# SwiGLU's result: transposing it in 32x32 blocks on VectorE and GpSimd instead of on TensorE

## The chip, the cores and the metric
The kernel runs on one core of one Trainium2 chip. A core has five engines that work side by side: TensorE (matrix products; PE in the profile, with its weight loads as PEld), VectorE (DVE), ScalarE (ACT), GpSimd (POOL) and SyncE (SP, whose queue issues the loads here). The metric is the device time of one execution in microseconds (us), the median of several runs.

## The reference, cut to what matters
One decoder layer on 256 tokens with D = 2048: a SwiGLU FFN (half step), a token mixer, and a second SwiGLU FFN (half step). Each sub-layer has a norm before and behind it, modulated by vectors (adaLN) that come from a product of c with w_ada.

```python
def swiglu(h, w_gate, w_up, w_down):
    return (jax.nn.silu(h @ w_gate) * (h @ w_up)) @ w_down

x = sublayer(x, 0, ffn(0), 0.5)
x = sublayer(x, 1, mixer, 1.0)
x = sublayer(x, 2, ffn(1), 0.5)
```

D_FF is 5632, so each FFN has three weight matrices of 46 MB in float32. All inputs are float32.

## The kernel before, in words
**Three products for one.** A float32 matrix product is made of three products of fp32r operands: each operand is split into a high part (a cast) and a low part (the operand less the high part). `mm3` (L333) issues them on L334, L335 and L336. For a weight tile, `split_w` (L308) has ScalarE cast the raw tile to wh (L315) and VectorE subtract it to get wl (L316); for an activation, `split_act` does the same (L369, L370).

**Weights.** `load_w` (L302) loads a raw tile of 128 x 2 x 512 numbers (2 k-chunks of 128 rows, 512 columns; 512 KB) through SyncE's queue into the pool rawp, tag "raw", which has 8 buffers. wh and wl have 4 buffers each (pool wsp). `w_tiles` goes through a weight matrix in such tiles; I call the work on one raw tile a step. After each step it calls `pump()` (L285), which advances the first of the pending pieces of work by one `yield`, and `side[0].step()`, which advances the adaLN sums by a certain rate. `flush()` runs all that is pending to its end.

**The adaLN sums.** `ada_sums` loads tiles of w_ada into the same 8 raw buffers and VectorE adds them up, scaled by the activated c (L171). Most of them lie in the first FFN, where the rate is about 0.66 tiles for each step.

**An FFN.** D_FF is cut into 11 blocks of 512 columns, and these into three groups (`supers`): 4, 4 and 3 blocks. For a block, the gate and the up product are made token by token into two PSUM banks each (`proj_tok`: tokens on partitions, 128 x 512 for each of two token tiles t); that is 8 steps for each product, fewer in the first FFN, where part of the sums was made ahead. Then `swiglu_evac` or, with sums made ahead, `swiglu_sum` makes silu(gate) * up as two tiles gts[t] of 128 tokens x 512 columns. Those pieces are pending, and are pumped during the steps of the next block: the multiplications behind its first step, the transposition behind its third and fourth. The down product needs the result with columns on partitions, so `to_g` (L532) transposes it: for each half of the 512 columns four transposes of 128x128 on TensorE (L538) into a PSUM bank, and then `split_act` into g, high and low. When all blocks of a group have their g, the down product runs over them, four quarters of 512 output columns each.

**What sets the order.** The program is written in order, and a planner in the framework puts the instructions of each engine's queue in their order when the program is built, by its own reckoning of when each is ready; waits between engines are put in by it. Buffers belong to tags: raw (8), t2 (6, used for sg and gt of SwiGLU, for g_post, and other short-lived tiles), wh and wl (4).

Of the kernel before, what the change touches and what calls it, by code (L numbers as in the profile page):

```python
# [8 lines left out]
F32 = mybir.dt.float32  # L9
# [5 lines left out]
P = 128  # L15
D = 2048
S = 256
NT = S // P
# [14 lines left out]
def tile_layer(  # L33
# [6 lines left out]
    nc = tc.nc  # L40
# [14 lines left out]
    rawp = ctx.enter_context(tc.tile_pool(name="rawp", bufs=8))  # L55
# [9 lines left out]
    def nm(s):  # L65
        uid[0] += 1
        return f"{s}_{uid[0]}"

    def ps():
        return psp.tile([P, 512], F32, tag="ps", name=nm("ps"))  # L70

    def t2(shape=(P, 512), dtype=F32):
        return tp.tile(list(shape), dtype, tag="t2", name=nm("t2"))
# [203 lines left out]
    pending = []  # L277

    def later(fn, *args):
        def one():  # L280
            fn(*args)
            yield
        pending.append(one())
# [11 lines left out]
    def flush():  # L295
        while pending:
            pump()
# [35 lines left out]
    def mm3(o, lh, ll, rh, rl, start, stop):  # L333
        nc.tensor.matmul(o, lh, rh, start=start, stop=False, skip_group_check=True)  # L334
        nc.tensor.matmul(o, lh, rl, start=False, stop=False, skip_group_check=True)  # L335
        nc.tensor.matmul(o, ll, rh, start=False, stop=stop, skip_group_check=True)  # L336
# [20 lines left out]
    def proj_tok(src, c0, begun=None, w=512, segs=FULL, banks=None, first=0):  # L357

        if begun is not None:
            banks, segs = begun[0], FULL[begun[1]:]  # L360
        banks = banks or [ps(), ps()]
        last = segs[-1][0] + segs[-1][1] - 1
        for k, wh, wl in w_tiles(src, segs, c0, w=w):
            for t in range(NT):
                tok_mm(k, wh, wl, t, banks[t][:, 0:w], first, last)
        return banks

    def split_act(dh, dl, src):
        act = nc.scalar.copy(dh, src)  # L369
        return nc.vector.tensor_tensor(out=dl, in0=src, in1=dh.bitcast(F32), op=ALU.subtract), act  # L370


    def parts():

        p = small((P, 8), "parts")
        nc.gpsimd.memset(p[:, 3:4], EPS)
        return p

    def sumsq(p, q, src):
        junk = t2()  # L380
        nc.scalar.activation(junk, src, AF.Square, scale=float(D) ** -0.5, accum_out=p[:, q + q // 3:q + q // 3 + 1])  # L381
# [81 lines left out]
    def early_w(src, c0, w):  # L463


        if src is None:
            return None
        tiles = []
        for half, h in enumerate((hh, hl)):
            raw = load_w(src, 2 * half, c0, w)  # L470
            v = h[:, 8:16, :].rearrange("p (a j u) s -> p a j (u s)", a=2, j=2)
            wh, wl = split_w(raw[:, :, 0:w], v, w)
            tiles += [(2 * half + j, wh[:, j, :], wl[:, j, :]) for j in range(2)]
        return tiles
# [54 lines left out]
        return banks, 2  # L529


    def to_g(g, gts):  # L532
        for i in range(2):
            pg = ps()
            for j in range(2):
                for t in range(NT):
                    m = 2 * i + j
                    nc.tensor.transpose(pg[:, j * S + t * P:j * S + (t + 1) * P], gts[t][:, m * P:(m + 1) * P], ident)  # L538
            split_act(g.t[:, 0, 2 * i:2 * i + 2, :], g.t[:, 1, 2 * i:2 * i + 2, :],
                      pg.rearrange("p (k s) -> p k s", s=S))  # L540
            yield

    def swiglu_evac(g, gb, ub):
        gts = []
        for t in range(NT):
            sg, gt = t2(), t2()
            nc.scalar.activation(sg, gb[t], AF.Silu)
            nc.vector.tensor_tensor(out=gt, in0=sg, in1=ub[t], op=ALU.mult)
            gts.append(gt)
        yield  # L550
        yield
        yield from to_g(g, gts)

    def swiglu_sum(gb, ub, part):

        pv = part.t.rearrange("p k s -> p (k s)")
        gts = []
        for t in range(NT):
            sg, gt = t2(), t2()
            nc.vector.tensor_tensor(out=sg, in0=pv[:, t * 512:(t + 1) * 512], in1=gb[t], op=ALU.add)  # L560
            nc.scalar.activation(sg, sg, AF.Silu)
            nc.vector.tensor_tensor(out=gt, in0=pv[:, 1024 + t * 512:1024 + (t + 1) * 512], in1=ub[t], op=ALU.add)
            nc.vector.tensor_tensor(out=gt, in0=sg, in1=gt, op=ALU.mult)
            gts.append(gt)
        part.free()
        g = Slot((P, 2, 4, S), F32R)

        def rest():
            yield
            yield  # L570
            yield from to_g(g, gts)

        pending.append(rest())
        return g

    def ffn(idx, supers, begun, xin, nxt, nxt_src=None, nxt_c0=None, nxt_w=512):

        y = None
        yp = [parts() for _ in range(NT)]

        def evac_y(si, q, t, bank):
            ys = y[t].t[:, q * 512:(q + 1) * 512]
            if si == 0:
                nc.scalar.copy(ys, bank)
            else:
                nc.vector.tensor_tensor(out=ys, in0=ys, in1=bank, op=ALU.add)  # L586
            if si == len(supers) - 1:
                sumsq(yp[t], q, ys)

        for si, blocks in enumerate(supers):  # L590
            gs = []
            n = len(blocks)
            for b, segs, part, banks in blocks:
                if si == 0 and begun is not None and not gs:
                    gb = proj_tok(w_ff_gate[idx], b * FB, begun)
                    ub = proj_tok(w_ff_up[idx], b * FB)
                elif part is not None:
                    gb = proj_tok(w_ff_gate[idx], b * FB, segs=segs, first=segs[0][0])
                    ub = proj_tok(w_ff_up[idx], b * FB, segs=segs, first=segs[0][0])
                    flush()  # L600
                    gs.append(swiglu_sum(gb, ub, part))
                    continue
                else:
                    gb = proj_tok(w_ff_gate[idx], b * FB, segs=segs, banks=banks and banks[0])
                    ub = proj_tok(w_ff_up[idx], b * FB, segs=segs, banks=banks and banks[1])
                flush()
                gs.append(Slot((P, 2, 4, S), F32R))
                pending.append(swiglu_evac(gs[-1], gb, ub))
            if y is None:
                y = [Slot((P, D)) for _ in range(NT)] if xin[0].__class__ is Half else [Half(t) for t in range(NT)]  # L610
            rows = [(4 * i, 4, 4 * b[0]) for i, b in enumerate(blocks)]

            def mms(k, wh, wl, t):
                g = gs[k // 4].t
                mm3(banks[t], g[:, 0, k % 4, t * P:(t + 1) * P], g[:, 1, k % 4, t * P:(t + 1) * P],
                    wh, wl, k == 0, k == 4 * n - 1)

            for q in range(4):
                banks = [ps(), ps()]
                if si == len(supers) - 1 and q == 2:  # L620
                    for s_ in xin:
                        s_.t
                if si == len(supers) - 1 and q == 3:
                    flush()
                    if side[0] is not None:
                        side[0].drain()
                    early = early_w(nxt_src, nxt_c0, nxt_w)
                    kept, slots = hold(w_ff_down[idx], rows, q * 512, NW if nxt is None else 3)

                    def last_mm(t):  # L630
                        for k, wh, wl in kept:
                            mms(k, wh, wl, t)

                    return boundary(last_mm, lambda t: evac_y(si, q, t, banks[t]), lambda t: times_gg(y, t, q), xin, y, yp, slots + gs,
                                    early, 1, nxt, nxt_src, nxt_c0, nxt_w)
                else:
                    for k, wh, wl in w_tiles(w_ff_down[idx], rows, q * 512):
                        for t in range(NT):
                            mms(k, wh, wl, t)
                    for t in range(NT):  # L640
                        later(evac_y, si, q, t, banks[t])
                        if si == len(supers) - 1:
                            later(times_gg, y, t, q)
            if si < len(supers) - 1:
                for g in gs:
                    g.free()
# [72 lines left out]
    for bs, n in (((0, 1, 2, 3, 4), 1), ((5, 6), 2), ((7,), 3)):  # L719
        first.until(n - 1)  # L720
        for b in bs:
            part = Slot((P, 8, S))
# [32 lines left out]
    blocks = [(4718, 410), (4308, 410), (3896, 412), (3484, 412), (G0, 412)]  # L755
# [387 lines left out]
```

## Time and profile before

| | |
|---|---|
| median of 3 runs | 1872.65 us (1872.63 to 1873.1) |
| the profiled execution | 1873.27 us |
| its span, first to last instruction | 1871.5 us |
| granted TensorE clock, mean | 0.999 |
| TensorE busy | 1821.6 us (97%) |
| VectorE busy | 1366.2 us (73%) |
| ScalarE busy | 853.0 us (46%) |
| GpSimd busy | 17.8 us (1%) |
| DMA, mean over the span | 267 GB/s |

The first FFN lies between about 20 and 780 us, the mixer up to about 1140 us, the second FFN behind it. A row with x is a group of instructions with their count. Busy times of an engine are those of its instructions; matmuls are pipelined, so a matmul of 0.39 us starts 0.23 us behind the one before it. An engine executes its queue in order, and an instruction that waits keeps those behind it waiting.

### The profile page before, as it was taken

The numbers are of one execution on the slowest core, as the hardware profiler recorded it, in microseconds if no ns is written. First come the engines' busy times: TensorE is split into PE (matmuls) and PEld (weight loads), VectorE is DVE, ScalarE is ACT, GpSimd is POOL, SyncE is SP. The second block draws the span as 40 slices with busy tenths as digits, with TensorE's granted clock in tenths as the row PEclk, the third lists the DMA queues.
The fourth block names the chain that finished last, engine by engine and source line by source line (L and its number), as shares of the span: only waits on it lengthen the run. The fifth ranks groups of instructions, "written<-read, shape, count | busy, mean of one in ns | idle before, by whom it ended". The sixth has DMA issues, their size and how long they took to land.

```text
span 1871.5 us, 23045 instructions
## 1 busy us (share of the span) xinstructions
PE 1821.6 (97%) x8493; PEld 1522.8 (81%) x8493; DVE 1366.2 (73%) x1483; ACT 853.0 (46%) x1058; POOL 17.8 (1%) x40
## 2 busy tenths in 40 slices
PE   3999999999999999999999999999999999999998
PEld 2888888888888888799988887888888888888886
DVE  6788798788987888868898987555556555556455
ACT  3545444444443444655545446444444444334443
POOL 0000000000000000000000000000000000000000
PEclk9999999999999999999999999999999999999999
DMA  9999889989899999588689994776777776677652
GB/s 356 335 361 346 306 297 319 317 311 321 291 335 322 340 304 340 183 240 280 219 287 310 355 344 140 221 221 213 228 228 220 222 224 217 217 228 219 187 191 90
DMA packets 232617, 499.82 MB, mean 267 GB/s; under 512 B 16828, under 2 KB 28332, under 8 KB 231992
## 3 DMA queue, kind: packets, MB, share of 16 engines
q1 hardware_dynamic: 232504, 498.36, 80.0%
q8 instruction: 66, 1.08, 0.2%
q14 instruction: 47, 0.39, 0.1%
HBM read 496.19 MB, written 2.10 MB: 266 GB/s over the span
## 4 chain that ended last, share of the span: by engine, by line
PE 86%; issue 8%; DVE 3%; DMA 2%; POOL 1%; ACT 0%; DVEq 0%; POOLq 0%; ACTq 0%
PE ps L334 28%; PE ps L335 28%; PE ps L336 28%; DVE acc L171 1%; PE ps L538 1%; DMA raw<-in_w_ff_up_dram 1%; DVE wl L316 1%; DMA raw<-in_w_ada_dram 0%; POOL rstd L387 0%; DMA xt<-in_x_dram 0%; DMA raw<-in_w_ff_gate_dram 0%; PE ps L930 0%; POOL brs L808 0%; PE ps L436 0%; PE ps L230 0%
## 5 line engine op out<-in xcount | busy, mean ns | idle before, releaser
L316 DVE TENSOR_TENSOR wl<-raw,wh 128x1024 fp32r<-128x1024 f32 (+2 forms) x637 | 768.6, 1210 | 453.7 <-ACT wh L315 453.0
L315 ACT CAST wh<-raw 128x1024 fp32r<-128x1024 f32 (+2 forms) x637 | 662.7, 1043 | 865.3 <-PE ps L336 742.5
L334 PE MATMUL ps<-wh,hh 128*128 128x512 f32 (+2 forms) x1680 | 652.1, 390 | 3.0 <-ACT hh L369 2.4
L335 PE MATMUL ps<-wl,hh 128*128 128x512 f32 (+2 forms) x1680 | 649.4, 387 | 1.2 <-DVE wl L316 1.2
L336 PE MATMUL ps<-wh,hl 128*128 128x512 f32 (+2 forms) x1680 | 649.7, 387 | 0.0
L334 PEld LDWEIGHTS ps<-wh,hh 128*128 128x128 f32 x1680 | 316.2, 189 | 62.2 <-ACT hh L369 3.0
L335 PEld LDWEIGHTS ps<-wl,hh 128*128 128x128 f32 x1680 | 316.6, 188 | 61.2 <-DVE wl L316 2.6
L336 PEld LDWEIGHTS ps<-wh,hl 128*128 128x128 f32 x1680 | 316.1, 188 | 60.4
L171 DVE SCALAR_TENSOR_TENSOR acc<-raw,cs,acc 128x1024 f32<-128x1024 f32 x270 | 345.1, 1278 | 0.8 <-DVE parts L385 0.4
L334 PE MATMUL ps<-wh,big 128*128 128x512 f32 x804 | 314.8, 392 | 0.0
L335 PE MATMUL ps<-wl,big 128*128 128x512 f32 x804 | 313.3, 390 | 0.2 <-DVE wl L316 0.2
L336 PE MATMUL ps<-wh,big 128*128 128x512 f32 x804 | 313.3, 390 | 0.0
L335 PEld LDWEIGHTS ps<-wl,big 128*128 128x128 f32 x804 | 151.1, 188 | 31.6 <-DVE wl L316 1.1
L336 PEld LDWEIGHTS ps<-wh,big 128*128 128x128 f32 x804 | 151.0, 188 | 31.6
L334 PEld LDWEIGHTS ps<-wh,big 128*128 128x128 f32 x804 | 150.9, 188 | 30.7
L680 ACT COPY big<-ps 128x512 f32<-128x512 f32 x32 | 18.7, 589 | 45.4 <-PE ps L336 44.3
L334 PE MATMUL ps<-hh,wh 128*128 128x256 f32 x128 | 37.6, 294 | 0.0
L370 DVE TENSOR_TENSOR big<-ps,big 128x512 fp32r<-128x512 f32 x52 | 35.5, 683 | 1.3 <-ACT big L369 1.2
L336 PE MATMUL ps<-hh,wl 128*128 128x256 f32 x128 | 36.2, 283 | 0.0
L335 PE MATMUL ps<-hl,wh 128*128 128x256 f32 x128 | 36.2, 283 | 0.0
L369 ACT CAST big<-ps 128x512 fp32r<-128x512 f32 x52 | 30.1, 578 | 0.0
L381 ACT ACTIVATE t<-xt 128x512 f32<-128x512 f32 x32 | 20.0, 626 | 17.8 <-DVE xt L586 9.8
(196 smaller groups left out, 742.6 us busy)
## 6 DMA issues: line engine op xcount, KB each, us to landing
raw<-in_w_ada_dram SPq DMA_DIRECT2D x224, 512.0 KB, 5.4
raw<-in_w_ff_gate_dram SPq DMA_DIRECT2D x176, 512.0 KB, 4.6
raw<-in_w_ff_up_dram SPq DMA_DIRECT2D x176, 512.0 KB, 4.5
raw<-in_w_ff_down_dram SPq DMA_DIRECT2D x176, 512.0 KB, 5.2
raw<-in_w_ada_dram SPq DMA_DIRECT2D x128, 256.0 KB, 5.4
raw<-in_w_in_dram SPq DMA_DIRECT2D x48, 512.0 KB, 5.0
raw<-in_w_out_dram SPq DMA_DIRECT2D x32, 512.0 KB
raw<-in_w_in_dram SPq DMA_DIRECT2D x24, 412.0 KB, 5.1
```

The lines of the kernel that those rows point to most:

```text
L171: ins = nc.vector.scalar_tensor_tensor(a, raw[:, j, :, :], cs[:, k:k + 1], a, op0=ALU.mult, op1=ALU.add)
L315: behind(nc.scalar.copy(wh, rawv), floor[1])
L316: last_split[0] = nc.vector.tensor_tensor(out=wl, in0=rawv, in1=wh.bitcast(F32), op=ALU.subtract)
L334: nc.tensor.matmul(o, lh, rh, start=start, stop=False, skip_group_check=True)
L335: nc.tensor.matmul(o, lh, rl, start=False, stop=False, skip_group_check=True)
L336: nc.tensor.matmul(o, ll, rh, start=False, stop=stop, skip_group_check=True)
L369: act = nc.scalar.copy(dh, src)
L370: return nc.vector.tensor_tensor(out=dl, in0=src, in1=dh.bitcast(F32), op=ALU.subtract), act
L381: nc.scalar.activation(junk, src, AF.Square, scale=float(D) ** -0.5, accum_out=p[:, q + q // 3:q + q // 3 + 1])
L538: nc.tensor.transpose(pg[:, j * S + t * P:j * S + (t + 1) * P], gts[t][:, m * P:(m + 1) * P], ident)
L680: nc.scalar.copy(part.t.rearrange("p k s -> p (k s)")[:, u * 1024 + i * 512:u * 1024 + (i + 1) * 512], banks[i])
```

## The change
For all blocks of a group but the last, `to_g_blocks` takes the place of `to_g`. VectorE transposes each 128x512 tile gts[t] in one instruction, in blocks of 32x32, which leaves each block on the partitions that it came from. GpSimd then copies the blocks to the partitions where they belong: for each of 4 x 4 pairs of source and target partition groups one copy of 32 partitions x 256 numbers, 16 in all. Then come four yields, and the two splits, which read the SBUF tile gf instead of a PSUM bank. tr and gf are tiles of the tag "raw", of the size of a raw tile. The transposes and the copies stand one pump behind the multiplications, the splits at the fifth and sixth pump behind that. The last block of each group goes through `to_g` as before.

```diff
+    def to_g_blocks(g, gts):
+        tr = rawp.tile([P, NT, 4, 4, 32], F32, tag="raw", name=nm("tr"))
+        gf = rawp.tile([P, 4, NT, 4, 32], F32, tag="raw", name=nm("gf"))
+        for t in range(NT):
+            nc.vector.transpose(tr[:, t].rearrange("p m q r -> p (m q r)"), gts[t])
+        for b in range(4):
+            for q in range(4):
+                nc.gpsimd.tensor_copy(gf[q * 32:(q + 1) * 32, :, :, b, :].rearrange("p m t r -> p t m r"),
+                                      tr[b * 32:(b + 1) * 32, :, :, q, :])
+        for _ in range(4):
+            yield
+        for i in range(2):
+            split_act(g.t[:, 0, 2 * i:2 * i + 2, :], g.t[:, 1, 2 * i:2 * i + 2, :],
+                      gf[:, 2 * i:2 * i + 2].rearrange("p m t b r -> p m (t b r)"))
+            yield
...
-    def swiglu_evac(g, gb, ub):
+    def swiglu_evac(g, gb, ub, blocks):
...
         yield
-        yield
-        yield from to_g(g, gts)
...
+        if blocks:
+            yield from to_g_blocks(g, gts)
+        else:
+            yield
+            yield from to_g(g, gts)
...
-                    gs.append(swiglu_sum(gb, ub, part))
+                    gs.append(swiglu_sum(gb, ub, part, len(gs) + 1 < n))
...
-                pending.append(swiglu_evac(gs[-1], gb, ub))
+                pending.append(swiglu_evac(gs[-1], gb, ub, len(gs) < n))
```

`swiglu_sum` takes the same flag and branches in the same way.

## Rows read from the trace of the kernel before

**Rows 1.** The page: busy time, share of the span, instructions of each engine.
```profile
PE 1821.6 (97%) x8493; PEld 1522.8 (81%) x8493; DVE 1366.2 (73%) x1483; ACT 853.0 (46%) x1058; POOL 17.8 (1%) x40
```
**Rows 2.** Busy time by stretch (us), granted clock, DMA share, GB/s.
```profile
200.00:300.00 100.00, 100.00 (x475) 82.42 (x474) 89.95 (x101) 47.84 (x57) 0.00 (x0) 1.00 0.86 290
...
400.00:500.00 100.00, 100.00 (x466) 82.30 (x465) 88.06 (x96) 44.11 (x48) 0.00 (x0) 1.00 0.90 305
...
1300.00:1500.00 200.00, 200.00 (x895) 165.64 (x894) 111.67 (x103) 86.80 (x93) 0.00 (x0) 1.00 0.72 222
```
**Rows 3.** Waits of the engines and of SyncE's queue: us, times, longest.
```profile
ACT wh L315 <- PE ps L336: 742.5, 465, 2.4
...
SPq L304 <- DVE wl L316: 895.7, 463, 20.6
```
**Rows 4.** Timeline, TensorE around four transposes: start, us, engine, line, operation.
```profile
228.78 0.39 PE L335 MATMUL ps<-wl,hh 128*128 128x512 f32 x1
...
229.00 0.39 PE L336 MATMUL ps<-wh,hl 128*128 128x512 f32 x1
...
229.24 0.60 PE L538 MATMUL ps<-ident,t 128*128 128x128 f32 x4
...
229.91 0.40 PE L335 MATMUL ps<-wl,hh 128*128 128x512 f32 x1
```
**Rows 5.** Groups by line and shape: count | busy us, mean ns of one.
```profile
L316 DVE TENSOR_TENSOR wl<-raw,wh 128x1024 fp32r<-128x1024 f32 x599 | 730.5, 1222 | 435.3 <-ACT wh L315 434.7
...
L171 DVE SCALAR_TENSOR_TENSOR acc<-raw,cs,acc 128x1024 f32<-128x1024 f32 x270 | 345.1, 1278 | 0.8 <-DVE parts L385 0.4
...
L369 ACT CAST big<-ps 128x512 fp32r<-128x512 f32 x52 | 30.1, 578 | 0.0
L538 PE MATMUL ps<-ident,t 128*128 128x128 f32 x176 | 26.3, 272 | 0.0
...
L182 DVE STREAM_TRANSPOSE t<-acc 128x512 f32<-128x512 f32 x22 | 14.6, 691 | 0.1
...
L369 ACT CAST hh<-t 128x512 fp32r<-128x512 f32 x14 | 8.3, 621 | 0.1
```
**Rows 6.** Timeline, second FFN: a block's two SiLUs and its multiplications.
```profile
1197.34 0.60 ACT L547 ACTIVATE t<-ps 128x512 f32<-128x512 f32 x1 [0.98 <-PE ps L336]
...
1218.01 0.59 ACT L547 ACTIVATE t<-ps 128x512 f32<-128x512 f32 x1
...
1219.29 1.28 DVE L548 TENSOR_TENSOR t<-t,ps 128x512 f32<-128x512 f32 x2
```
**Rows 7.** Timeline: a group's last multiplications, a g_post load, its consumer.
```profile
1308.25 1.28 DVE L548 TENSOR_TENSOR t<-t,ps 128x512 f32<-128x512 f32 x2
...
1309.18 0.35 SPq L224 DMA_DIRECT2D t<-in_g_post_dram  x1
...
1430.20 0.68 DVE L225 TENSOR_TENSOR acc<-acc,t 1x512 f32<-1x512 f32 x1
```
**Rows 8.** Timeline, first FFN: VectorE at a block's end, and its transposes.
```profile
433.56 0.68 DVE L562 TENSOR_TENSOR t<-big,ps 128x512 f32<-128x512 f32 x1
...
437.16 0.68 DVE L563 TENSOR_TENSOR t<-t,t 128x512 f32<-128x512 f32 x1
437.76 1.22 DVE L316 TENSOR_TENSOR wl<-raw,wh 128x1024 fp32r<-128x1024 f32 x1
...
441.97 0.60 PE L538 MATMUL ps<-ident,t 128*128 128x128 f32 x4
```
**Rows 9.** Groups of GpSimd by shape.
```profile
L843 POOL TENSOR_SCALAR_AFFINE_SELECT big<-onesr 128x128 f32<-128x128 f32 x1 | 0.3, 292 | 1.1 <-PE ps L336 1.1
```
**Rows 10.** Timeline, mixer: GpSimd and VectorE side by side.
```profile
895.80 0.69 DVE L898 TENSOR_TENSOR t<-t,t 128x512 f32<-128x512 f32 x1
...
907.86 0.64 POOL L891 TENSOR_SCALAR_AFFINE_SELECT t<-t 128x512 f32<-128x512 f32 x1 [10.88 <-ACT big L903]
...
908.00 1.04 DVE L898 TENSOR_TENSOR t<-t,t 128x512 f32<-128x512 f32 x1
```

More of the change, by code (lines that the diff above doesn't have):

```diff
@@ L550, in swiglu_evac, with swiglu_sum @@
         yield
-        yield
-        yield from to_g(g, gts)
-    def swiglu_sum(gb, ub, part):
+        if blocks:
[3 more added lines that the diff above has]
+            yield from to_g(g, gts)
+    def swiglu_sum(gb, ub, part, blocks):
         pv = part.t.rearrange("p k s -> p (k s)")
@@ L569, in rest @@
             yield
-            yield
-            yield from to_g(g, gts)
+            if blocks:
+                yield from to_g_blocks(g, gts)
+            else:
+                yield
+                yield from to_g(g, gts)
         pending.append(rest())
```

## The prediction
> **What bounds the kernel now.** I read the page's engine table first. TensorE is busy 97% of the span, VectorE 73%, ScalarE 46%, GpSimd 1% [rows 1]. The shares differ by stage, so the stretches come next [rows 2]: in the first FFN (200 to 300 us, 400 to 500 us) and in the second (1300 to 1500 us) TensorE is busy throughout, at a granted clock of 1.00. VectorE differs: 0.90 and 0.88 of the two stretches of the first FFN, 0.56 in the second, because the first also carries most of the adaLN sums. The DMA share is 0.86 to 0.90 against 0.72. Then the waits [rows 3]: ScalarE's cast of a weight tile waits 742.5 us for TensorE to give a buffer back, and the load queue 895.7 us for VectorE to release a raw tile. So everything runs ahead until its buffers are full, and TensorE sets the pace. What leaves TensorE's queue shortens the run, as long as VectorE, ScalarE and the loads keep their lead. That lead is four tiles (wsp), and a tile feeds one step: 2 k by 2 t by 3 products, 12 matmuls at 0.227 us from start to start, 2.72 us.
>
> **What is removed.** Four transposes stand between two matmuls at 229.00 and 229.91 [rows 4]. The two starts lie 0.91 us apart with one further matmul between them, which alone would make 2 x 0.227 = 0.45 (the pace from 228.78 to 229.00 is 0.22). So four transposes cost 0.46 us, though each is shown at 0.27: they overlap. There are 176 [rows 5], eight for each of 22 blocks. The six groups have 4, 4, 3, 4, 4, 3 blocks and their last ones stay, so 16 blocks lose theirs: 32 fours x 0.45 = 14.4 us, half of it in each FFN. All of it is on the path, since TensorE is.
>
> **What is added and moved.** Per block: two VectorE block transposes, 16 GpSimd copies of 32 partitions x 256 elements, and two splits that read SBUF instead of PSUM.
> The split: ScalarE's cast takes 621 ns from SBUF and 578 from PSUM [rows 5], so 43 ns x 32 = 1.4 us on an engine that waits for TensorE in every step: nothing. VectorE's subtraction behind it keeps its shape: I take no difference, with the same 43 ns as the bound either way.
> The transposes: the same form stands in the rows at 691 ns [rows 5]; 32 x 0.69 = 22 us of VectorE. In the second FFN its idle 44% covers them. In the first they count against 10 to 12% of slack.
> The copies: the trace has none. The nearest GpSimd rows that read and write SBUF take 0.29 us for 128 elements [rows 9] and 0.64 for 512 [rows 10]; between them 256 elements come to about 0.41. I take that; the ends are 0.29 and 0.64. Sixteen: 6.6 us alone (4.6 to 10.2). Only 32 partitions work at a time, and whether crossing partitions costs extra no row shows.
>
> **Two costs that the diff hides.**
> (1) Order. The first SiLU of a block runs in mid-block, as soon as the gate product is complete (1197.34), though its code stands behind the whole up product; the second, equally ready, runs only at the block's end (1218.01), beside the first multiplication (1219.29) [rows 6]. Between them in program order lies the tile that this multiplication fills. Likewise the g_post load needs no data; its consumer runs at 1430.20, yet it is issued at 1309.18, behind the last multiplications of a group (from 1308.25) [rows 7], which fill the tiles just ahead of it. I read this as buffers of one tag being handed out in program order when the queues are ordered. The new tiles tr and gf have the tag of the weight loads. So the weight tiles that follow them in the program fall behind the block transposes in VectorE's order, where the subtraction of wl runs ahead of TensorE today by the lead. In the first FFN at the block end 433.8 (the transposes at 441.97 less three steps) VectorE does five sums and products from 433.56 [rows 8], 0.60 apart, and then two transposes at 0.69: to 437.9. The delayed wl (1.22) ends at 439.1, with an adaLN sum (1.28 [rows 5]) ahead of it, in two of three cases, at 440.4. TensorE wants it at 433.8 + 2 x 2.72 + 0.23 = 439.5. So 0 to 0.9 us late, 0.6 on average; today that subtraction lies in front of the five. In the second FFN, with two products instead of five operations, it is 2 us early: no loss.
> (2) The port. A VectorE operation on two SBUF operands and a GpSimd operation that reads SBUF do not run together: L898 takes 0.69 us beside one GpSimd instruction, and 1.04 when it starts at 908.00 while one of 0.64 that began at 907.86 still runs [rows 10]. So a VectorE operation can lose up to 0.41 us behind a copy. If half of the 16 copies collide in full, 3.3 us per block, with the transposes 4.7. Three changed blocks in 100 us make 14 us against the 10 to 12 free: 2 to 4 us too many, 0.7 to 1.4 per block.
> (1) and (2) use up the same lead, so they are not added: 0.9 us per block in the first FFN, x 8 = 7.2 us (ends: 0, and about 4 per block, below). Second FFN: 0 (its 44% is 19 us in a block of 16 steps, 44 us, four times the 4.7).
> The Trainium skill, SBUF — State Buffer, "Who interferes with whom", says the same more strictly: the shared pair is an exclusive lock, and the second to issue blocks until the first is done. Rows 10 agree for VectorE behind GpSimd; what it does when both queues are full is the second rival.
>
> **Sum.** -14.4 + 7.2 = -7.2 us. The profiled execution took 1873.27 us (span 1871.5 and 1.8 around it), 0.6 above the median 1872.65; from the median: 1865.5. Its own range is 1859 to 1869.5.
>
> **Rivals.**
> *All of it hidden, 1858.3.* For it: ScalarE and VectorE wait in every step for TensorE, the second FFN has room for everything, and copies on different partitions might overlap. Against: 88 to 90% VectorE in the first FFN. 1872.65 - 14.4. Chance 0.20.
> *ScalarE stands in front of the split, slower.* The split waits for the last copy, and the casts of the next weight tiles are queued behind it. Place: the eight changed blocks of the first FFN. If each copy must let one VectorE operation (about 1.25 us) pass, the 16 last 16 x 1.66 = 27 us instead of 6.6, from 4 us to 31 us behind the block end. The split's place in the program is five steps behind the transposes; if the casts up to the seventh step are queued ahead of it (an estimate), TensorE has work for 7 x 2.72 = 19 us. Once ScalarE stands, VectorE runs dry and the copies run alone, so the end moves from 31 to about 23, and the next wl is ready 3 us later, at 26: at worst 7 us per block, 4 taken. 8 x 4 - 14.4 = +17.6: 1890. It decides from 14.4 / 8 = 1.8 us per block, that is when the copies end later than some 18 us behind the block end. Against: in the second FFN VectorE leaves 0.44 x 2.72 = 1.2 us in each step free, three copies, and so the chain ends in time. Chance 0.29.
> *The loads, no change.* tr and gf take two of the eight buffers that the loads use, in a stage where the DMA share is already 0.86 to 0.90 [rows 2]. If that costs the DMA 4 to 5 us in a block of 12 steps (33 us) with 3.3 us to spare, TensorE loses some 1.8 per block and the saving is gone: 1872. Against: weight loads wait for buffers today, not for the DMA engines [rows 3]. Chance 0.15.
>
> **How the numbers follow.** My forecast has 0.36. About 0.2% (3.7 us) is what a measurement of this kernel can tell from no change. Faster: 0.20 from the first rival, 0.30 of the forecast, 0.03 of the loads: 0.53. Same: 0.06, 0.09 and 0.01 of the standing ScalarE: 0.16. Slower: 0.28 and 0.03: 0.31. Range: 1857 (all hidden, with a little measurement spread) to 1888; it leaves out the upper half of the second rival, 0.15.
>
> **What would show it.** The groups of TensorE's transposes: 48 in to_g instead of 176. Right: TensorE without gaps in the second FFN, 7 us shorter; in the first, short waits of matmuls for wl two or three steps behind a block's end. VectorE's wl rows longer than 1.22 us only while copies run; copies longer than 0.41 us where VectorE is full. Wrong: matmuls that wait for wh behind a split that waits for GpSimd (second rival), casts that wait for a raw load in the first FFN (third), or single copies far above 0.64 us even in the second FFN, where then no cover would hold.

## The result: 7.3% slower

The changed kernel takes 2009.97 us (median of 4 runs, 2008.84 to 2010.85) against 1872.7: 1.073 times as long, 95% interval 1.072 to 1.074. The prediction said 1865.5, in a range of 1857 to 1888. It was wrong in sign, and the loss of 137 us is nearly ten times the 14.4 us that were to be saved.

The page after, its row of engines (as rows 1) and the granted clock in 40 slices of the span:
```profile
PE 1857.4 (92%) x8365; PEld 1534.3 (76%) x8365; DVE 1383.3 (69%) x1515; ACT 849.0 (42%) x1058; POOL 135.5 (7%) x296
...
PEclk9999989988899999999999999999999999999999
```
The 128 transposes are gone (8365 instructions against 8493). But TensorE is idle for 2008.6 - 1857.4 = 151.2 us of the span, against 1871.5 - 1821.6 = 49.9 [rows 1]: 101.3 more. And it is busy for 35.8 us more, with 14.4 us of work less: some 50 us go into work that ran slower. The two make the 137.1 us by which the span grew.

The stretches of rows 2, after (same columns):
```profile
200.00:300.00 100.00, 76.27 (x321) 60.27 (x320) 64.41 (x76) 33.98 (x43) 21.55 (x48) 0.90 0.59 196
400.00:500.00 100.00, 85.65 (x352) 67.94 (x352) 68.89 (x74) 32.46 (x35) 16.03 (x32) 0.90 0.67 240
1300.00:1500.00 200.00, 191.23 (x821) 156.50 (x821) 104.97 (x95) 80.40 (x87) 14.31 (x32) 0.97 0.66 212
```
In the first FFN VectorE falls from 0.90 to 0.64 and the DMA share from 0.86 to 0.59. No engine has become the bound there: everybody waits for somebody. The second FFN loses too, where the prediction saw room for everything.

Waits after (us in total, times, longest), of the engines and of SyncE's queue:
```profile
ACT wh L315 <- PE ps L336: 585.6, 364, 3.6
...
ACT big L369 <- POOL gf L541: 182.2, 16, 14.8
...
PE ps L334 <- ACT wh L315: 94.2, 17, 9.3
...
SPq L304 <- DVE wl L316: 820.9, 438, 20.6
...
SPq L304 <- POOL gf L541: 117.2, 15, 8.8
```
The second line is new: in each of the 16 blocks ScalarE stands with its split for 11.4 us on average, until GpSimd's last copy. The third is its effect: 17 waits of TensorE for a weight cast, some 5.5 us each. The last line is new as well: the load queue stands for the copies.

One block of the second FFN shows all of it (timeline: start, us, engine, line, operation, idle before and releaser; sorted by start):
```profile
1303.26 16.60 SPq L304 DMA_DIRECT2D raw<-in_w_ff_gate_dram  x4
...
1304.60 0.59 ACT L565 ACTIVATE t<-ps 128x512 f32<-128x512 f32 x1
...
1306.36 1.05 ACT L315 CAST wh<-raw 128x1024 fp32r<-128x1024 f32 x1 [1.18 <-PE ps L336]
...
1309.76 1.30 DVE L538 STREAM_TRANSPOSE tr<-t 128x512 f32<-128x512 f32 x2
...
1310.98 1.18 DVE L316 TENSOR_TENSOR wl<-raw,wh 128x1024 fp32r<-128x1024 f32 x1
...
1311.17 7.78 POOL L541 COPY gf<-tr 32x256 f32<-32x256 f32 x16 [43.19 <-DVE tr L538]
...
1316.82 0.39 PE L336 MATMUL ps<-wh,hl 128*128 128x512 f32 x1
...
1318.99 1.14 ACT L369 CAST big<-gf 128x512 fp32r<-128x512 f32 x2 [11.57 <-POOL gf L541]
...
1320.03 3.93 ACT L315 CAST wh<-raw 128x1024 fp32r<-128x1024 f32 x4
...
1321.12 0.79 PE L334 MATMUL ps<-wh,hh 128*128 128x512 f32 x1 [3.92 <-ACT wh L315]
...
1322.38 0.79 PE L335 MATMUL ps<-wl,hh 128*128 128x512 f32 x1 [0.47 <-DVE wl L316]
...
1327.24 0.42 PE L334 MATMUL ps<-wh,hh 128*128 128x512 f32 x1
...
1327.73 0.39 PE L336 MATMUL ps<-wh,hl 128*128 128x512 f32 x1
```
ScalarE casts one weight tile behind the second SiLU (1306.36) and then both splits are next in its queue. The copies, all but the first without hindrance (7.78 us for the 16), are done at 1318.95, but until then no further weight is cast. The same holds in all 16 blocks: behind the last SiLU one weight cast stands ahead of the split, or none (four blocks). TensorE uses up its tiles at 1317. From 1316.82 to 1327.73 it starts 15 matmuls, 15 x 0.227 = 3.4 us of work in 10.9: 7.5 us lost. Of these 4.1 pass before the first one starts, 1.0 behind that one (its wl is late too), and 2.4 in the eleven that follow 0.44 apart.

Why 0.44: the stretches of 2 us around it (columns as above; the third from the end is the granted clock, the next the DMA share):
```profile
1316.00:1318.00 2.00, 1.20 (x6) 0.66 (x4) 0.00 (x0) 0.00 (x0) 1.83 (x5) 1.00 0.00 0
1318.00:1320.00 2.00, 0.00 (x0) 0.00 (x0) 0.36 (x1) 1.01 (x2) 0.87 (x3) 1.00 0.02 2
1320.00:1322.00 2.00, 0.79 (x1) 0.28 (x1) 1.83 (x3) 2.00 (x4) 0.00 (x0) 0.61 0.90 250
1322.00:1324.00 2.00, 1.62 (x4) 1.33 (x5) 2.00 (x3) 1.96 (x3) 0.00 (x0) 0.50 1.05 394
...
1328.00:1330.00 2.00, 2.00 (x10) 1.65 (x9) 1.23 (x1) 0.52 (x1) 0.00 (x0) 1.00 1.00 351
```
TensorE had been idle for 3.92 us; then the clock was granted at 0.50, its lower level (1.2 GHz), and came back to 1.00 behind some 6 us of work. The loads had stopped altogether (DMA share 0.00): the queue stood.

### The profile page after: what moved, and what is told of

The parts are those of the page before. It is cut to its first block, busy times and chain, and to the rows that moved or that the text cites. A ratio compares the mean times of both kernels' runs of the same rounds, so it can differ in the third digit from the quotient of the medians.

```text
span 2008.6 us, 23105 instructions
## 1 busy us (share of the span) xinstructions
PE 1857.4 (92%) x8365; PEld 1534.3 (76%) x8365; DVE 1383.3 (69%) x1515; ACT 849.0 (42%) x1058; POOL 135.5 (7%) x296
## 5 line engine op out<-in xcount | busy, mean ns | idle before, releaser
L334 PE MATMUL ps<-wh,hh 128*128 128x512 f32 (+2 forms) x1680 | 662.1, 399 | 96.6 <-ACT wh L315 94.2
L335 PE MATMUL ps<-wl,hh 128*128 128x512 f32 (+2 forms) x1680 | 667.2, 397 | 9.5 <-DVE wl L316 9.3
L336 PE MATMUL ps<-wh,hl 128*128 128x512 f32 (+2 forms) x1680 | 662.6, 394 | 0.0
L334 PEld LDWEIGHTS ps<-wh,hh 128*128 128x128 f32 x1680 | 325.6, 195 | 166.4 <-ACT wh L315 101.7
L335 PEld LDWEIGHTS ps<-wl,hh 128*128 128x128 f32 x1680 | 325.1, 194 | 84.7 <-DVE wl L316 22.6
L336 PEld LDWEIGHTS ps<-wh,hl 128*128 128x128 f32 x1680 | 324.8, 193 | 62.0
L541 POOL COPY gf<-tr 32x256 f32<-32x256 f32 x256 | 117.7, 460 | 1296.2 <-DVE tr L538 1077.9
L370 DVE TENSOR_TENSOR big<-gf,big 128x512 fp32r<-128x512 f32 x32 | 20.8, 688 | 110.0 <-ACT big L369 110.0
L369 ACT CAST big<-gf 128x512 fp32r<-128x512 f32 x32 | 18.2, 615 | 182.2 <-POOL gf L541 182.2
L566 DVE TENSOR_TENSOR t<-t,ps 128x512 f32<-128x512 f32 x28 | 18.8, 685 | 26.8 <-PE ps L336 26.3
L704 ACT COPY big<-ps 128x512 f32<-128x512 f32 x32 | 18.7, 589 | 43.5 <-PE ps L336 42.5
```

The costliest lines, as they stand in the source:

```text
L541: nc.gpsimd.tensor_copy(gf[q * 32:(q + 1) * 32, :, :, b, :].rearrange("p m t r -> p t m r"), tr[b * 32:(b + 1) * 32, :, :, q, :])
L704: nc.scalar.copy(part.t.rearrange("p k s -> p (k s)")[:, u * 1024 + i * 512:u * 1024 + (i + 1) * 512], banks[i])
```

## The experiments

Three theories. **A**: the split stands in ScalarE's queue ahead of casts that TensorE needs, because tr and gf, tiles of the load tag, push the weight tiles behind them back in the program's order. **B**: the port; copies and VectorE hinder each other and eat VectorE's lead. **C**: the loads; tr and gf hold two of the eight buffers until the copies and the splits are done, and SyncE's queue, which hands them out in order, stands behind them. The kernel before ran beside each of them, at 1873.0 to 1873.3 us.

**1. Order and memory, in both FFNs.** e1 orders each split behind the weight cast of the step in which it is written; e2 gives tr and gf tags of their own, in the memory of two load buffers; e0 is the kernel before with those six; e4 is e1 and e2 together.
```diff
+            behind(act, last_cast[0])        # e1, e4: split's cast behind last wh cast
...
-    rawp = ... tile_pool(name="rawp", bufs=8)
+    rawp = ... tile_pool(name="rawp", bufs=6)   # e0, e2, e4
...
-        tr = rawp.tile([P, NT, 4, 4, 32], F32, tag="raw", ...)
+        tr = blkp.tile([P, NT, 4, 4, 32], F32, tag="tr", ...)   # e2, e4; gf likewise
```


> The changed kernel, with one thing added: each of the two splits behind the copies is ordered behind the weight cast of the step in which it is written (four casts now stand between the second SiLU and the first split on ScalarE, instead of one). Theory A (ScalarE stands in front of the split, with the next weight casts queued behind it): the copies end 7.8 us after they start, TensorE has tiles for about 11 us, so the stalls and the drops of the clock go: 1858 to 1870 us. Theory B (the port that VectorE and GpSimd dispute, and VectorE's lost lead): copies and transposes are the same, so about as slow as the change, 1980 to 2010. Theory C (two of the eight load buffers taken away, loads late): buffers are the same, 1980 to 2010.

> The changed kernel with tr and gf in two buffers of their own and six for the loads (the same memory). By the program's queues, three casts now stand between the second SiLU and the splits, instead of one, because the weight tiles no longer queue for buffers behind tr and gf. Theory A: copies end about 10 us behind the block's last product, tiles for 8 us are ahead: a short stall or none, 1858 to 1885. Theory B: 1980 to 2010. Theory C, if the number of load buffers is what counts: six for the loads at all times, so slower still than the change or equal, 2000 to 2030.

> The kernel before with six load buffers instead of eight, nothing else. Theory A: loads have room to spare in the second FFN (issue to cast 13 us against 5 us of transfer) and little in the first: 1872 to 1885. Theory C: a loss of 60 us or more, 1930 or slower. Theory B says nothing of it: 1872 to 1875.

> The changed kernel with tr and gf in buffers of their own (six load buffers) and the splits ordered behind the weight cast of their step. The theory by now has two parts: A, the split stands on ScalarE in front of weight casts; C, tr and gf lie among the load buffers, so that the loads behind them wait until the copies have ended. Both are taken away here, and the kernel before with six load buffers took 1893.2. If A and C are all: 1893.2 - 14.4 = 1879, up to 1885. If the port and VectorE's lost lead in the first FFN (part B of the prediction) cost what was forecast, 7 us or more on top: 1886 to 1905. If A was not what e2 still lost: about 1939 as e2.


Measured: e1 1965.5 (ratio 1.048 to 1.051), e2 1939.2 (1.034 to 1.037), e0 1893.2 (1.009 to 1.012), e4 1935.6 (1.032 to 1.035). None of the three theories alone foretold e1, and e2 and e0 fell between the expectations as well. In e1 A has a share (44 us come back), and what is left is something else. In e1's first FFN it is now the loads that are late (timeline, and one line of the waits):
```profile
473.23 13.69 SPq L305 DMA_DIRECT2D raw<-in_w_ff_gate_dram  x2
...
475.24 11.29 POOL L543 COPY gf<-tr 32x256 f32<-32x256 f32 x16 [32.97 <-DVE tr L540]
...
490.34 1.04 ACT L316 CAST wh<-raw 128x1024 fp32r<-128x1024 f32 x1 [12.38 <-DMA raw<-in_w_ff_gate_dram]
```
```profile
SPq L305 <- POOL gf L543: 166.0, 15, 12.1
```
SyncE issues two loads in 13.7 us, done when the copies are, and ScalarE waits 12.38 us for a raw tile; the split behind it waits for nothing. In e2 and e4 the second FFN is clean (TensorE 200.00 of 200 us busy at 1300 to 1500), but the first is not: two buffers fewer, and the split still stands 9.58 us behind copies that take 10.4 to 13.2 us a block there. In six of the eight blocks there, e4 has no more casts ahead of the first split than e2 (two, in one block three), so its 3.6 us hardly test A in the first FFN. Two waits of 1.46 and 1.60 us follow, and the clock falls (matmuls at 0.63):
```profile
441.68 0.62 ACT L372 CAST big<-gf 128x512 fp32r<-128x512 f32 x1 [9.58 <-POOL gf L544]
...
443.29 0.50 PE L337 MATMUL ps<-wh,hh 128*128 128x512 f32 x1 [1.46 <-ACT wh L317]
445.40 0.50 PE L338 MATMUL ps<-wl,hh 128*128 128x512 f32 x1 [1.60 <-DVE wl L319]
...
446.60 0.63 PE L339 MATMUL ps<-wh,hl 128*128 128x512 f32 x1
```

**2. The added work, read by nobody.** The kernel before makes its result with TensorE's transposes, and the block transposes and copies run beside it: in e3 into tiles of the load tag, in e10 into own tags (six load buffers).
```diff
         yield
+        (block transposes and copies of to_g_blocks, gf unread)
         yield from to_g(g, gts)
```


> The kernel before with the added work and nobody waiting for it: TensorE's transposes stay and feed the splits, and the block transposes and the 16 copies of each of the 16 blocks are made as well, into tr and gf of the tag raw, which nothing reads. Theory A: 1872 to 1880 (the 14.4 us of TensorE's transposes are back, nothing stands). Theory B: the quarrel over the port is all there, 1872.7 plus about 150: 2000 to 2030. Theory C: tr and gf take the load buffers as in the change, 1990 to 2030.

> The kernel before with six load buffers, and beside it the block transposes and the copies of the change, in own tags, which nobody reads; TensorE's transposes stay and make the result. So only the work of VectorE and GpSimd is added: no split waits for it and no load buffer is held. Six buffers alone made 1893. Theory 'place of the split': what e4_late_own lost against 1893 - 14.4 = 1879 (57 us) came through the split, so the added work alone costs little: 1891 to 1900. Theory 'port': the copies and the transposes slow VectorE in the first FFN by themselves: 1925 to 1950. A value between shares it out.


Measured: e3 1964.5 (1.048 to 1.051), e10 1899.7 (1.012 to 1.016). Without a single instruction that waits for the added result, e3 loses 91 us, a value that none of the three theories foretold. Its waits, SyncE's queue first:
```profile
SPq L304 <- POOL gf L541: 211.0, 15, 18.6
...
ACT wh L315 <- DMA raw<-in_w_ff_gate_dram: 146.0, 35, 18.9
ACT big L369 <- PE ps L552: 118.5, 22, 9.8
```
The first two lines are C: the queue stands for the copies, and ScalarE for raw tiles (28.4 us for this matrix in the kernel before). The third is A in another form: ScalarE stands with its split, now for TensorE's own transposes, and in 15 of the 16 blocks none or one weight cast is ahead of it, where e10 has two to four in 14. So the load tag moves the casts even where nobody reads its tiles, and how the 91 us divide between A and C isn't shown. e10 costs 6.5 us over the six buffers' 1893.2: that is B and VectorE's added transposes by themselves, in a kernel with six load buffers; with eight they were not measured apart. Its groups by line say who pays:
```profile
L317 DVE TENSOR_TENSOR wl<-raw,wh 128x1024 fp32r<-128x1024 f32 x599 | 737.0, 1234 | 425.6 <-ACT wh L316 421.8
...
L542 POOL COPY gf<-tr 32x256 f32<-32x256 f32 x256 | 214.9, 840 | 1102.8 <-DVE tr L539 1092.8
```
A copy takes 840 ns in place of 460 in the change; the wl subtraction 1234 in place of 1222 [rows 5], 599 x 12 ns = 7 us of VectorE in the whole run. The port quarrel is GpSimd's loss.

**3. The second FFN alone.** Here one large piece of SBUF is free, so tr and gf can have memory of their own with all eight load buffers kept. e6: load tag, as in the change. e11: the same with the split ordered late. e5: own memory. e7: own memory and late.
```diff
-   gs.append(swiglu_sum(gb, ub, part, len(gs) + 1 < n))
+   gs.append(swiglu_sum(gb, ub, part, False))                     # all four
-   pending.append(swiglu_evac(gs[-1], gb, ub, len(gs) < n))
+   pending.append(swiglu_evac(gs[-1], gb, ub, idx == 1 and len(gs) < n))
...
-        tr = rawp.tile([P, NT, 4, 4, 32], F32, tag="raw", ...)     # gf likewise
+        st = Slot((P, 2, 1024))                                    # e5, e7
+        tr, gf = st.t[:, 0], st.t[:, 1]                            # rearranged
```


> The change in the second FFN alone (8 of the 16 blocks), tr and gf among the load buffers as in the change; the first FFN as before. A with C: each changed block of the second FFN took 51.0 us in the changed kernel and 44.4 before, 8 x 6.5 = 52 more: 1920 to 1930. The prediction's own view (loss only where VectorE is full, in the first FFN): 1865.

> As e6_ffn1_raw, but tr and gf lie in one of the large buffers that are free in the second FFN, so that all eight load buffers stay with the loads; nothing is ordered by hand. A with C: the queue then has three casts ahead of the splits, and loads never wait for copies: 1872.7 - 8 x 0.9 = 1865.5, with 0 to 2 us lost per block at most (1865 to 1875). If the copies' length alone were the cause, or the port: no better than e6_ffn1_raw, about 1925.

> The change in the second FFN only, tr and gf in the load tag as in the change, with the splits ordered behind the weight cast of their step. Three times stand beside it: 1927 with the splits where the change puts them (e6_ffn1_raw), 1865 with the same order of the splits and tr and gf in memory of their own (e7_ffn1_slot_late). Theory 'the split in front of the casts' (all of the loss of 61 us in this FFN comes through ScalarE's order): 1865 to 1872. Theory 'the load queue stands' as the other half of it: the loads behind gf still come late and TensorE waits for them in some blocks; e1_split_late showed 12 us of such waits in this FFN with 14 us of lower clock behind them, so 1880 to 1890. If the load queue alone made the loss: 1910 or more.

> As e5_ffn1_slot, with the splits ordered behind the weight cast of their step as well (one cast comes between the two splits). A with C: no stall left, 1865 to 1867, equal to e5_ffn1_slot or up to 5 us faster. If the block transposes and copies cost VectorE's lead even where it is 44% idle: 1870 or more.

| second FFN only | split as in the change | split late |
|---|---|---|
| load tag | e6 1927.45 (1.028 to 1.030) | e11 1886.77 (1.006 to 1.009) |
| own memory | e5 1866.16 (0.995 to 0.998) | e7 1864.95 (0.994 to 0.997) |

This square divides the loss of the second FFN: 61 us between e6 and e5 by the tag alone. The order of the split gives back 41 of them (A). The 22 left between e11 and e7 are put down to the loads (C) by the waits: in this FFN ScalarE waits 29.7 us for raw tiles of w_gate and w_up in e11; in e7 its profile lists no such wait. In e11 the queue takes 17.49 us for three loads, and ScalarE, with enough casts ahead of the split, waits for a raw tile instead:
```profile
1216.29 17.49 SPq L305 DMA_DIRECT2D raw<-in_w_ff_gate_dram  x3
...
1236.65 1.04 ACT L316 CAST wh<-raw 128x1024 fp32r<-128x1024 f32 x1 [3.13 <-DMA raw<-in_w_ff_gate_dram]
...
1237.75 0.50 PE L336 MATMUL ps<-wh,hh 128*128 128x512 f32 x1 [2.08 <-ACT wh L316]
```
In e5, three casts stand between the second SiLU and the split, where the change has one:
```profile
1216.46 0.59 ACT L567 ACTIVATE t<-ps 128x512 f32<-128x512 f32 x1
1218.23 1.06 ACT L315 CAST wh<-raw 128x1024 fp32r<-128x1024 f32 x1 [1.18 <-PE ps L336]
1220.95 1.06 ACT L315 CAST wh<-raw 128x1024 fp32r<-128x1024 f32 x1 [1.66 <-PE ps L336]
1223.67 1.05 ACT L315 CAST wh<-raw 128x1024 fp32r<-128x1024 f32 x1 [1.66 <-PE ps L336]
1230.87 1.14 ACT L369 CAST big<-big 128x512 fp32r<-128x512 f32 x2 [6.15 <-POOL big L542]
```
ScalarE still stands 6.15 us, and nobody misses it. The copies begin at 1176.85, 1220.29 and 1263.82 in three successive blocks: 43.5 us per block, against 44.5 before (from 1219.29 to 1308.25 are two blocks [rows 6, 7]) and 51.0 in the change (from 1260.21 to 1311.17). e7 is the fastest version and beats the kernel before by 0.3 to 0.6%; its copies take 9.8 to 10.9 us a block, slowed by VectorE, and no cost of that shows. The difference from e5 is within the measurement.

**4. The split still later.** e8 is e4, e9 is e1, each with six yields instead of four ahead of the splits.
```diff
-        for _ in range(4):
+        for _ in range(6):
             yield
```


> As e4_late_own (own tags for tr and gf, six load buffers, splits ordered behind the weight cast of their step), but the splits stand two steps later in the program (six yields instead of four). In e4 the splits of the first FFN still stood 9 to 10 us on ScalarE, because a block's copies took 10 to 13 us beside a full VectorE. Theory 'place of the split': two steps are 5.4 us and two more casts ahead, so the wait shrinks to about 4 us, less than TensorE's lead of four tiles; the waits of matmuls for wh and wl in the first FFN go and with them the clock drops behind them: 1879 to 1892 (1893 for six buffers, less up to 14.4). Theory 'port and buffers' (what is lost there is VectorE's time beside the copies, and the loads): the later place changes nothing, 1925 to 1940.

> As e1_split_late (tr and gf in the load tag with eight buffers, splits ordered behind the cast of their step), but with the splits two steps later (six yields). Theory 'the load queue stands' (SyncE waits for the copies and the splits to release the two buffers): gf holds its buffer 5 us longer, so the time doesn't fall: 1960 to 1985. Theory 'place of the split' (ScalarE standing for the copies is all that matters): the wait of the split in the first FFN goes, 1890 to 1930.


Measured: e8 1918.6 (1.023 to 1.026), e9 1979.0 (1.055 to 1.059). With the load tag a later split costs 13.5 us more, as C expected, since gf keeps its buffer longer. With own tags it gains 17, a value between the two expectations and nearer to that of port and buffers. ScalarE's wait for the copies falls from 109.8 us (e4) to 60.0, but e8 stays 40 us above 1879 (six buffers, less 14.4). In that remainder waits for wh and wl of 1 to 2 us alternate with clock drops in the first FFN; how it divides between the split, the short loads and VectorE stays open. Own memory beside all eight load buffers, which would tell, was not run in the first FFN.

## Why the prediction was wrong

**The bound: right.** Where the cover holds, TensorE sets the pace and what leaves its queue is saved: 0.45 per four transposes, 16 fours in the second FFN, makes 7.2; e5 shows 6.9 (4.5 to 9.2, from its ratio).

**Durations: right.** Block transposes 0.69 (690 ns measured), splits from SBUF 615 ns against 581 from PSUM, subtraction 688 against 685. A copy was put at 0.41; alone it takes 0.39 to 0.40, 0.43 from start to start. Groups of the change by line:
```profile
L541 POOL COPY gf<-tr 32x256 f32<-32x256 f32 x256 | 117.7, 460 | 1296.2 <-DVE tr L538 1077.9 <-DMA raw<-in_w_ada_dram 208.3
...
L538 DVE STREAM_TRANSPOSE tr<-t 128x512 f32<-128x512 f32 x32 | 20.9, 690 | 0.0
L370 DVE TENSOR_TENSOR big<-gf,big 128x512 fp32r<-128x512 f32 x32 | 20.8, 688 | 110.0 <-ACT big L369 110.0
...
L369 ACT CAST big<-gf 128x512 fp32r<-128x512 f32 x32 | 18.2, 615 | 182.2 <-POOL gf L541 182.2
```

**Cost (1), order: here the prediction failed.** Its rule held: buffers of one tag are handed out in program order, and weight tiles behind tr and gf fall back. It drew this for VectorE alone: wl does come behind the block transposes (1309.76, then 1310.98), and in this block that costs nothing. The same rule holds for ScalarE's casts of those tiles, and they fall behind the splits, which wait for the whole chain of copies. The sum has the split on ScalarE at "nothing", by its duration, without asking what stands behind it in the queue. Only the second rival asked, and there an estimate, "the casts up to the seventh step are queued ahead", took the place of the rule; in the change one cast is, or none, in e5 three in seven of the eight blocks. The rule holds for SyncE's loads as well. So the second FFN's "no loss" was 61 us of loss (e6 against e5), 41 of them through ScalarE's order. Its free VectorE time made the copies fast, and it didn't help: when they begin, at 1311.17, TensorE has tiles until 1317.05, 5.9 us, and 16 copies take 7.8.

The working for VectorE at a block's end also puts its five operations 0.60 apart without a gap. In the trace before, an adaLN sum of 1.28 us stands among them, and the fifth starts at 437.16 [rows 8], not at 435.96; no run shows what that alone would change.

**Cost (2), the port: right in kind, wrong in payer.** It was put at 3.3 us of VectorE per block, up to 0.41 for a collision. Measured (e3, 436 to 443 us): a VectorE operation beside a copy takes 1.40 to 1.42 in place of 1.22 to 1.28, and the copy 1.29 to 1.30 in place of 0.40. In a whole run it is 6.5 us (e10); that is near the 7.2 which the sum had for both costs, but by luck: the working had VectorE as the payer. The trace before had the payer: the GpSimd instruction that starts together with L898 at 895.80 [rows 10] takes 1.18 us, where the other takes 0.64:
```profile
895.80 1.18 POOL L891 TENSOR_SCALAR_AFFINE_SELECT t<-t 128x512 f32<-128x512 f32 x1 [43.32 <-DVE t L886]
```

**The rival that ScalarE stands in front of the split (0.29): the right mechanism**, with the wrong place (the first FFN only), the wrong point of decision (copies that end 18 us behind the block end; in the block shown 10.6 were enough, from 1308.40, where VectorE's products start, to 1318.95) and so the wrong price: 4 us a block for eight, against 7.5 a block in the second FFN and, from 2010 - 1927 + 7, about 90 us in all for the first, the loads' share included.

**The rival of the loads (0.15): right that they cost, for another reason.** I looked at the share of the DMA engines. What counted is the order of the queue that issues: it stands for one buffer, and the DMA goes to 0.00 meanwhile. It costs 22 us in the second FFN alone (e11 against e7). In e1, where the split waits for no copy in seven of the eight blocks of the first FFN, 92 us over the kernel before are left in all, and this rival had room for 14.

**Not priced at all: the clock.** Each stall of 4 to 9 us is followed by matmuls 0.43 apart in place of 0.227. In the trace after, from 50 us on, 198 matmuls of 128x512 last 0.55 us or more, against 12 before: 186 x 0.2 us explain some 37 of the 50 by which TensorE's remaining work grew. The rest I did not assign.

## What to carry to other kernels

A tile allocated from the tag of a prefetch stream doesn't only take a buffer. The load that needs this buffer next waits until the tile is released, with every load behind it in the queue; and on the engines that handle the stream, what comes later in it was queued later too, here ScalarE's casts behind the splits. Before moving work to an idle engine, write out, for each engine, which queue entries will stand behind the instruction that waits for the result, and compare the latency of the new chain (here 16 copies, 8 to 13 us) with the work that the bound engine has in store. Give the new tiles memory of their own first (e5); if the waiting instruction still stands in front of work that must not wait, place it later (e8 gained 17 us by that over e4, e7 nothing that shows over e5).

## What the runs showed of the hardware

- Copying across partitions costs GpSimd nothing extra that shows: in the block from 223.25 us of the change, all 16 pairs of source and target partitions take 0.39 to 0.40 us for 32 x 256 numbers.
- With both queues full, copies and two-operand VectorE operations take turns, one for one. Stretches of one block of e1 (columns as above; VectorE is the third, GpSimd the fifth):
```profile
475.20:481.75 6.55, 6.55 (x29) 4.95 (x28) 6.27 (x5) 1.05 (x1) 6.33 (x5) 1.00 0.15 57
481.75:486.60 4.85, 2.62 (x12) 1.84 (x10) 0.00 (x0) 0.00 (x0) 4.34 (x11) 1.00 0.00 0
```
  Five copies pass beside five VectorE operations, 1.3 us each; with VectorE idle eleven take 0.39 each. The loser is the engine with the short operations. A pair takes 1.33 us from start to start, where the two alone take 1.14 (e3, from 448.48 to 449.62) and 0.43. The exclusive lock that the Trainium skill describes (SBUF — State Buffer, "Who interferes with whom") agrees with the turns, but not with their length: one strictly behind the other would make 1.57.
- How long TensorE waited in one piece doesn't tell whether the clock falls. In e11 it stayed at 1.00 behind the wait of 2.08 us before 1237.75, and fell behind two shorter ones (stretch of 3 us, granted clock third from the end):
```profile
1283.70 0.51 PE L336 MATMUL ps<-wh,hh 128*128 128x512 f32 x1 [1.06 <-ACT wh L316]
1284.96 0.75 PE L337 MATMUL ps<-wl,hh 128*128 128x512 f32 x1 [0.75 <-DVE wl L318]
```
```profile
1286.00:1289.00 3.00, 3.00 (x10) 2.34 (x9) 2.98 (x3) 1.42 (x2) 0.00 (x0) 0.59 1.05 385
```
